# Seven-product weight forms by additions, two of them in transfers, and the scan's decay tiles for both heads of a feature block in one piece

## The chip, the cores and the metric

The kernel runs on one core of a Trainium2 chip, as one program of 52,322 recorded instructions. The metric is the device time of one execution in microseconds. The times shown for the kernel before are 2779.19 us (median of three), 2778.53 and 2781.94 us.

The engines are named as in the profile: PE is the matrix engine (PEld its weight loads), DVE the vector engine, ACT the scalar engine, POOL the GpSimd engine. SP issues transfers and computes nothing. Each engine works through its own list of instructions in order.

## What is computed

One residual block over 512 frames of 2048 channels. All operands are 32-bit floats.

```python
h = rmsnorm(x, norm1_w)
proj = einsum('bsd,de->bse', h, w_in)          # 2048 -> 22592 columns
q, k, v, g_ret, z, xbc, dt_raw, gate_r, gate_s = split(proj)
y_r = retention(q, k, v, positions) * silu(g_ret)
y_s = ssd(xbc, dt_raw, conv_w, conv_b, dt_bias, a_log, d_skip)
y_s = rmsnorm(y_s * silu(z), ssd_norm_w)
merged = sigmoid(gate_r) * (y_r @ w_br_ret) + sigmoid(gate_s) * (y_s @ w_br_ssd)
x = rmsnorm(x + merged @ w_out, norm_f_w)

# inside ssd, per chunk of frames (64 heads, 8 groups of B and C):
seg = acum[:, :, None] - acum[:, None, :]
decay = exp(where(causal, seg, -inf))
cb = einsum('blgn,bsgn->blsg', cc, bc)
y = einsum('blsg,blsgh,bsghp->blghp', cb, decay, xc)
```

## The kernel before

Nearly all of the work is the five big projections. Each is cut into **units** of 256 output columns by 512 frames over 2048 input channels. A unit is one call of `unit`, which calls `products`. There are 119 such units and a last one, written out by hand, which is done in two passes.

In a unit the 2048 channels are taken in eight steps of 256 (`k` in `range(NP)`). A step multiplies a 2 by 2 arrangement of 128x128 weight blocks by a 2 by 2 arrangement of 128x256 operand blocks. In 101 units (`SEVEN`) this is done with seven products of combined blocks in place of eight; in 18 units (`FOUR`, called plain) and the last one without combining. Each product is three matmuls on rounded halves (lines 202 to 204): high weights by high operand, high weights by low operand, low weights by high operand. A seven-product unit has 8 x 7 x 3 = 168 matmuls with 256 moving columns, a plain one 96 with 512.

Weights come in **pairs** of steps. One tile `wf` holds a pair: for each of its two steps seven slots of 128x128, of which slots 0 to 3 are loaded by SP (line 216, one transfer of 256 KB a step) and slots 4 to 6 are for combined blocks. In seven-product units DVE forms the combinations of both steps in three instructions: line 219 (two slots of each step, 128x512), then lines 221 and 222 (one slot of each step, 128x256 each). Then, for each step, ACT rounds the seven slots to `whi` (line 150) and DVE subtracts to get `wlo` (line 151). There are three buffers of `wf` (`FB`), seven of `whi` (`HB`), six of `wlo` (`LB`): a pair's load can be issued when the second `wlo` of the pair three before has been subtracted, and a rounding when PE is done with the weights seven steps before. All of this is issued at a higher priority than the work around it (`PRIO`), so the weights run ahead of PE. A scheduler fixes the order of each engine's list when the kernel is built.

The operand side (`operands`, with `combined` on POOL or DVE and `completed` on DVE) is formed in the same way, once for each projection: for `w_in` at the very start, where `POOL` forms combinations for seven of eight operand tiles, then for the branch outputs and the merged sum.

The stages, by the first loads of their weights: retention and its projections from the start to about 765 us, the SSD stage to about 2048 us, the three products of the branches to 2566 us, the output projection to the end.

In the SSD stage there are 32 feature blocks of 128 channels, that is, of two heads. For each head a tile `L` (128 x 4 x 128) is loaded with the running sums of that head spread over all partitions (line 643, one transfer of 256 KB), made into decays by ACT (four times line 645, once line 647), multiplied by `CB` on DVE (line 648), and used in four matmuls (line 650). These read 64 columns of weights, and the first head writes partitions 0 to 63 of the result, the second head 64 to 127. The hardware runs each of these matmuls as two, so a feature block has sixteen in the trace.

Of the kernel before, what the change touches and what calls it, by code (L numbers as in the profile page):

```python
# [16 lines left out]
P = 128  # L17
# [49 lines left out]
def constants():  # L67
# [7 lines left out]
    for h in range(NH):  # L75
# [17 lines left out]
SEVEN = (((0, 0, 1, 1), (1, 0, 3, 3), (1, 1, 0, 5)),  # L93
         ((2, 0, 5, 6), (2, 1, 4, 4)),
# [35 lines left out]
def hybrid_block(tc, A, out):  # L130
# [23 lines left out]
    def combined(f, eng):  # L154
        eng.tensor_tensor(f[:, 4, :], f[:, 0, :], f[:, 2, :], op=ALU.add)
        eng.tensor_tensor(f[:, 6, :], f[:, 0, :], f[:, 1, :], op=ALU.subtract)

    def completed(f, eng):
        eng.tensor_tensor(f[:, 5, :], f[:, 4, :], f[:, 1, :], op=ALU.subtract)
        eng.tensor_tensor(f[:, 0, :], f[:, 3, :], f[:, 5, :], op=ALU.subtract)  # L160
# [13 lines left out]
    def rows(src, i):  # L174
        return src[i * 256:(i + 1) * 256, :].rearrange("(r p) t -> p r t", p=P)

# [12 lines left out]
    def products(H, parts, pt, groups, PE=PE, after=None):  # L189
# [17 lines left out]
        for k in range(NP):  # L207
            with tc.high_priority(offset=PRIO):
                if k % 2 == 0:
# [8 lines left out]
                    if not plain:  # L218
                        DVE.tensor_tensor(f2[:, :, 4:6, :], f2[:, :, 1:3, :],  # L219
                                          f2[:, :, 0:1, :].to_broadcast([P, 2, 2, P]), op=ALU.subtract)  # L220
                        DVE.tensor_tensor(f2[:, :, 0, :], f2[:, :, 2, :], f2[:, :, 4, :], op=ALU.add)  # L221
                        DVE.tensor_tensor(f2[:, :, 6, :], f2[:, :, 3, :], f2[:, :, 0, :], op=ALU.subtract)  # L222
# [16 lines left out]
    def unit(H, parts, alt=False, plain=False):  # L239
# [7 lines left out]
        with tc.high_priority():  # L247
            if plain:
                for c in range(2):
                    ACT.copy(o[:, 2 * c:2 * c + 2, :], pt[2 * c][:, 0:1, :].to_broadcast([P, 2, 256]))  # L250
                    DVE.tensor_tensor(o[:, 2 * c, :], pt[2 * c][:, 1, :], o[:, 2 * c, :], op=ALU.add)
                    DVE.tensor_tensor(o[:, 2 * c:2 * c + 2, :], pt[2 * c + 1], o[:, 2 * c:2 * c + 2, :], op=ALU.add)
            else:
                p1, u = o[:, 0, :], o[:, 0:4:3, :]
                ACT.copy(p1, pt[0][:, 0, :])  # L255
                DVE.tensor_tensor(o[:, 1:3, :], pt[1], p1[:, None, :].to_broadcast([P, 2, 256]), op=ALU.add)  # L256
                DVE.tensor_tensor(u, o[:, 2:3, :].to_broadcast([P, 2, 256]), pt[2], op=ALU.subtract)
                DVE.tensor_tensor(o[:, 2, :], o[:, 0, :], pt[2][:, 1, :], op=ALU.subtract)
                DVE.tensor_tensor(u, pt[3], u, op=ALU.add)
# [297 lines left out]
    with tc.tile_pool(name="ssd", bufs=1) as sp:  # L557
# [30 lines left out]
        for g in range(NG):  # L588
# [14 lines left out]
            for jj in range(2):  # L603
# [5 lines left out]
                for e in range(2):  # L609
# [29 lines left out]
                    pi = att_tile()  # L639
                    for i in range(2):  # L640

                        L = sp.tile([P, TB, P], F32, name="L", bufs=2)
# [179 lines left out]
```

## Time and profile before

| | |
|---|---|
| median of three runs | 2779.19 us |
| the profiled execution | 2779.37 us |
| its span, first to last instruction | 2777.6 us |
| PE, DVE, ACT, POOL busy | 98%, 86%, 48%, 9% of the span |
| PE clock granted, mean | 0.991 |
| HBM read, written | 321.56 MB, 37.49 MB |
| packets of all transfer queues | 344,375 |

The profiled execution lies 1.8 us over its span and 0.2 us over the median, so sums made on the trace can be set against the median as they are. A matmul's duration in a row is from its entry to its modelled end, and matmuls overlap; the pace of PE is read from the distance of their starts. Rows of the timeline give start in us, duration in us, engine, line, operation, output and inputs by the program's names, and how many instructions a row merges. Rows by line and shape give count, busy us, mean ns of one, and the idle time just before them with what ended it. Rows of one stretch of time give each engine's busy us, the granted clock, the share of the 16 transfer engines' time that packets took, and GB/s.

### The profile page before, as it was taken

The numbers are of one execution on the slowest core, as the hardware profiler recorded it, in microseconds if no ns is written. First come the engines' busy times: TensorE is split into PE (matmuls) and PEld (weight loads), VectorE is DVE, ScalarE is ACT, GpSimd is POOL, SyncE is SP. The second block draws the span as 40 slices with busy tenths as digits, with TensorE's granted clock in tenths as the row PEclk, the third lists the DMA queues.
The fourth block names the chain that finished last, engine by engine and source line by source line (L and its number), as shares of the span: only waits on it lengthen the run. The fifth ranks groups of instructions, "written<-read, shape, count | busy, mean of one in ns | idle before, by whom it ended". The sixth has DMA issues, their size and how long they took to land.

```text
span 2777.6 us, 52322 instructions
## 1 busy us (share of the span) xinstructions
PE 2715.8 (98%) x20508; PEld 2586.4 (93%) x20508; DVE 2391.4 (86%) x3782; ACT 1336.1 (48%) x1905; POOL 253.1 (9%) x206
## 2 busy tenths in 40 slices
PE   6999999999999999999999999999999999999898
PEld 3899999999989999999999999999989989889797
DVE  8999888888869798898979899797989798898997
ACT  4344333333355555555565555465554343533453
POOL 4000000000000000000000000000021020111321
PEclk9999999999999999999999999999999999999999
DMA  3333333333333434343434434344465554556634
GB/s 125 99 103 104 97 109 103 103 92 103 103 111 114 134 122 133 104 128 117 135 121 135 135 109 126 119 129 120 129 199 168 162 179 137 167 179 194 217 117 137
DMA packets 344375, 362.48 MB, mean 131 GB/s; under 512 B 25664, under 2 KB 298304, under 8 KB 344128
## 3 DMA queue, kind: packets, MB, share of 16 engines
q1 hardware_dynamic: 323888, 325.32, 38.7%
q10 hardware_dynamic: 20240, 33.82, 3.3%
q8 instruction: 161, 2.64, 0.4%
q14 instruction: 86, 0.70, 0.1%
HBM read 321.56 MB, written 37.49 MB: 129 GB/s over the span
## 4 chain that ended last, share of the span: by engine, by line
PE 82%; DVE 8%; DMA 5%; issue 3%; ACT 1%; POOL 1%; SPq 0%; DVEq 0%; POOLq 0%; ACTq 0%
PE pb L204 23%; PE pb L203 23%; PE pb L202 23%; PE att L202 2%; PE att L204 2%; PE att L203 2%; DVE wlo L151 2%; PE att L650 2%; DMA wf<-in_w_in_dram 1%; PE att L536 1%; PE att L521 1%; DMA wf<-in_w_br_ssd_dram 1%; DVE hl L151 1%; PE pb L120 1%; PE att L654 1%
## 5 line engine op out<-in xcount | busy, mean ns | idle before, releaser
L203 PE MATMUL pb<-hl,whi 128*128 128x256 f32 (+1 forms) x5464 | 1601.1, 294 | 11.9 <-DVE hl L120 9.3
L202 PE MATMUL pb<-hh,whi 128*128 128x256 f32 (+1 forms) x5464 | 1596.8, 295 | 9.9 <-ACT hh L150 7.1
L204 PE MATMUL pb<-hh,wlo 128*128 128x256 f32 (+1 forms) x5464 | 1587.9, 294 | 6.0 <-DVE wlo L151 6.0
L150 ACT CAST whi<-wf 128x896 fp32r<-128x896 f32 (+1 forms) x968 | 824.5, 888 | 870.1 <-PE pb L203 396.6
L203 PEld LDWEIGHTS pb<-hl,whi 128*128 128x128 f32 x5464 | 1049.1, 192 | 34.6 <-DVE hl L120 11.0
L202 PEld LDWEIGHTS pb<-hh,whi 128*128 128x128 f32 x5464 | 1046.4, 192 | 33.8 <-ACT hh L150 8.4
L151 DVE TENSOR_TENSOR wlo<-wf,whi 128x896 fp32r<-128x896 f32 (+1 forms) x968 | 1011.8, 1056 | 71.9 <-PE pb L204 30.6
L204 PEld LDWEIGHTS pb<-hh,wlo 128*128 128x128 f32 x5464 | 1041.0, 192 | 28.1 <-DVE wlo L151 6.8
L219 DVE TENSOR_TENSOR wf<-wf 128x512 f32<-128x512 f32 x404 | 281.5, 697 | 159.1 <-DMA wf<-in_w_in_dram 118.8
L202 PE MATMUL att<-hh,whi 128*128 128x256 f32 (+1 forms) x768 | 227.0, 297 | 1.4 <-ACT whi L150 1.4
L203 PE MATMUL att<-hl,whi 128*128 128x256 f32 (+1 forms) x768 | 226.7, 297 | 0.0
L204 PE MATMUL att<-hh,wlo 128*128 128x256 f32 (+1 forms) x768 | 222.7, 297 | 2.0 <-DVE wlo L151 2.0
L221 DVE TENSOR_TENSOR wf<-wf 128x256 f32<-128x256 f32 x404 | 174.3, 432 | 4.0
L222 DVE TENSOR_TENSOR wf<-wf 128x256 f32<-128x256 f32 x404 | 174.0, 431 | 3.1
L202 PEld LDWEIGHTS att<-hh,whi 128*128 128x128 f32 x768 | 147.4, 192 | 6.0 <-ACT whi L150 2.0
L204 PEld LDWEIGHTS att<-hh,wlo 128*128 128x128 f32 x768 | 144.8, 191 | 7.0 <-DVE wlo L151 2.8
L203 PEld LDWEIGHTS att<-hl,whi 128*128 128x128 f32 x768 | 147.5, 192 | 3.9
L645 ACT ACTIVATE L<-L,sst 128x128 f32<-128x128 f32 x256 | 80.3, 394 | 70.3 <-DMA L<-A_d 40.6
L625 POOL TENSOR_TENSOR xl<-xd,sst 128x384 f32<-128x384 f32 x32 | 33.7, 1054 | 864.1 <-DVE xd L622 864.1
L255 ACT COPY o<-pb 128x256 f32<-128x256 f32 x89 | 33.0, 370 | 128.0 <-PE pb L204 117.8
L256 DVE TENSOR_TENSOR o<-pb,o 128x512 f32<-128x512 f32 x89 | 61.0, 685 | 36.2 <-PE pb L204 35.9
L542 POOL TENSOR_TENSOR rs<-rs,mhalf 128x1 f32<-128x1 f32 x32 | 23.9, 751 | 713.3 <-DVE rs L541 704.2
(230 smaller groups left out, 2133.4 us busy)
## 6 DMA issues: line engine op xcount, KB each, us to landing
wf<-in_w_in_dram SPq DMA_DIRECT2D x640, 256.0 KB, 3.1
wf<-in_w_br_ssd_dram SPq DMA_DIRECT2D x128, 256.0 KB, 3.5
wf<-in_w_out_dram SPq DMA_DIRECT2D x72, 256.0 KB, 3.2
wf<-in_w_in_dram SPq DMA_DIRECT2D x128, 128.0 KB, 2.5
L<-A_d SPq DMA_DIRECT2D x64, 256.0 KB, 3.4
wf<-in_w_br_ret_dram SPq DMA_DIRECT2D x64, 256.0 KB, 3.5
ys_d<-B ACTq DMA_DIRECT2D x32, 256.0 KB, 2.5
E<-E_d SPq DMA_DIRECT2D x64, 96.0 KB, 2.7
```

Source lines behind the costliest of these rows:

```text
L150: ACT.copy(dst_hi, src)
L151: DVE.tensor_tensor(dst_lo, src, dst_hi.bitcast(F32), op=ALU.subtract)
L202: PE.matmul(o, wh, xh, start=b not in started, stop=False, skip_group_check=True)
L203: PE.matmul(o, wh, xl, start=False, stop=False, skip_group_check=True)
L204: PE.matmul(o, wl, xh, start=False, stop=(k == NP - 1), skip_group_check=True)
L219: DVE.tensor_tensor(f2[:, :, 4:6, :], f2[:, :, 1:3, :], f2[:, :, 0:1, :].to_broadcast([P, 2, 2, P]), op=ALU.subtract)
L221: DVE.tensor_tensor(f2[:, :, 0, :], f2[:, :, 2, :], f2[:, :, 4, :], op=ALU.add)
L222: DVE.tensor_tensor(f2[:, :, 6, :], f2[:, :, 3, :], f2[:, :, 0, :], op=ALU.subtract)
L256: DVE.tensor_tensor(o[:, 1:3, :], pt[1], p1[:, None, :].to_broadcast([P, 2, 256]), op=ALU.add)
L625: POOL.tensor_tensor(xl, xd[:, :TB - 1], tail[:, :TB - 1, hs, None].to_broadcast([P, TB - 1, 2, 64]), op=ALU.mult)
L645: ACT.activation(L[:, c, :], L[:, c, :], AF.Relu, scale=-1.0, bias=At[:, c, h0 + i:h0 + i + 1])
L650: PE.matmul(pi[i * 64:(i + 1) * 64, c * P:(c + 1) * P], xd[:, c, i, :], L[:, c, :], start=True, stop=True)
```

## The change

It has four parts.

1. **Weight combinations.** The two sets of seven combinations (of weights and of operands) get other signs, so that on the weight side every combination is a sum. Slot 5 is loaded with a second copy of block 0 by a third transfer on SP's queue (new line 228, 128 KB for both steps). Then, for each step, one transfer issued by POOL (new line 230, `accum_op=ALU.add`) adds slots 1 and 2 into slots 0 and 5, within SBUF. DVE does the two that are left: slot 4 (new line 231) and slot 6 (new line 232), 128x256 each. The 128x512 instruction of line 219 is gone. Tables, signs on the operand side and signs where results are collected follow (`SEVEN`, `combined`, `completed`, `unit`, the last unit); their instructions keep engine and shape, except that in plain units ACT copies 256 columns in place of 512.
2. **Decay tiles.** `L` is one tile for both heads of a feature block, with one buffer, loaded in one transfer of 512 KB; the eight first activations are as before, the exponential and the product with `CB` are one instruction each over 1024 columns.
3. **Order of the matmuls on `L`.** The four positions are the outer loop and the two heads the inner one, so matmuls that write partitions 0 to 63 and 64 to 127 alternate.
4. **The order of the lists**, which the scheduler works out anew.

```diff
-SEVEN = (((0, 0, 1, 1), (1, 0, 3, 3), (1, 1, 0, 5)),
-         ((2, 0, 5, 6), (2, 1, 4, 4)),
+SEVEN = (((0, 0, 1, 1), (1, 0, 3, 3), (1, 1, 4, 5)),
+         ((2, 0, 5, 6), (2, 1, 0, 4)),
          ((3, 0, 6, 2), (3, 1, 2, 0)))
...
     def combined(f, eng):
-        eng.tensor_tensor(f[:, 4, :], f[:, 0, :], f[:, 2, :], op=ALU.add)
-        eng.tensor_tensor(f[:, 6, :], f[:, 0, :], f[:, 1, :], op=ALU.subtract)
+        eng.tensor_tensor(f[:, 4, :], f[:, 0, :], f[:, 2, :], op=ALU.subtract)
+        eng.tensor_tensor(f[:, 6, :], f[:, 0, :], f[:, 1, :], op=ALU.add)
...
+    def first_tiles(src, i):
+
+        return src[i * 256:(i + 2) * 256, :P].rearrange("(m r p) t -> p m r t", r=2, p=P)[:, :, 0, :]
...
                     if not plain:
-                        DVE.tensor_tensor(f2[:, :, 4:6, :], f2[:, :, 1:3, :],
-                                          f2[:, :, 0:1, :].to_broadcast([P, 2, 2, P]), op=ALU.subtract)
-                        DVE.tensor_tensor(f2[:, :, 0, :], f2[:, :, 2, :], f2[:, :, 4, :], op=ALU.add)
-                        DVE.tensor_tensor(f2[:, :, 6, :], f2[:, :, 3, :], f2[:, :, 0, :], op=ALU.subtract)
+
+                        SP.dma_start(out=f2[:, :, 5, :], in_=first_tiles(parts[0], k))
+                        for m in range(2):
+                            POOL.dma_start(out=f2[:, m, 0:6:5, :], in_=f2[:, m, 1:3, :], accum_op=ALU.add)
+                        DVE.tensor_tensor(f2[:, :, 4, :], f2[:, :, 0, :], f2[:, :, 2, :], op=ALU.add)
+                        DVE.tensor_tensor(f2[:, :, 6, :], f2[:, :, 4, :], f2[:, :, 3, :], op=ALU.add)
...
             if plain:
                 for c in range(2):
-                    ACT.copy(o[:, 2 * c:2 * c + 2, :], pt[2 * c][:, 0:1, :].to_broadcast([P, 2, 256]))
-                    DVE.tensor_tensor(o[:, 2 * c, :], pt[2 * c][:, 1, :], o[:, 2 * c, :], op=ALU.add)
+                    ACT.copy(o[:, 2 * c + 1, :], pt[2 * c][:, 0, :])
+                    DVE.tensor_tensor(o[:, 2 * c, :], pt[2 * c][:, 1, :], o[:, 2 * c + 1, :], op=ALU.subtract)
...
+                    L = sp.tile([P, 2, TB, P], F32, name="L")
+                    SP.dma_start(out=L.rearrange("p i c l -> p i (c l)"),
+                                 in_=A_d[hs, :].partition_broadcast(P))
                     for i in range(2):
-
-                        L = sp.tile([P, TB, P], F32, name="L", bufs=2)
-                        SP.dma_start(out=L.rearrange("p c l -> p (c l)"), in_=A_d[h0 + i].partition_broadcast(P))
                         for c in range(TB):
-                            ACT.activation(L[:, c, :], L[:, c, :], AF.Relu, scale=-1.0,
+                            ACT.activation(L[:, i, c, :], L[:, i, c, :], AF.Relu, scale=-1.0,
                                            bias=At[:, c, h0 + i:h0 + i + 1])
-                        ACT.activation(L, L, AF.Exp, scale=-1.0)
-                        DVE.tensor_tensor(L, L, CB, op=ALU.mult)
-                        for c in range(TB):
-                            PE.matmul(pi[i * 64:(i + 1) * 64, c * P:(c + 1) * P], xd[:, c, i, :], L[:, c, :],
+                    ACT.activation(L, L, AF.Exp, scale=-1.0)
+                    DVE.tensor_tensor(L, L, CB[:, None].to_broadcast([P, 2, TB, P]), op=ALU.mult)
+
+                    for c in range(TB):
+                        for i in range(2):
+                            PE.matmul(pi[i * 64:(i + 1) * 64, c * P:(c + 1) * P], xd[:, c, i, :], L[:, i, c, :],
                                       start=True, stop=True)
```

The scheduler's new lists at three places. First DVE's list in the products of the branches, where a unit of the second one begins; rows give line, operation, output and inputs with buffer numbers, so that a pair is known by the number of its `wf`. Before:

```order
L219 TENSOR_TENSOR wf_26146<-wf_26146 128x2x256
L151 TENSOR_TENSOR wlo_26068<-wf_26057,whi_26067 128x896
L221 TENSOR_TENSOR wf_26146<-wf_26146 128x2x128
L219 TENSOR_TENSOR wf_26202<-wf_26202 128x2x256
L222 TENSOR_TENSOR wf_26146<-wf_26146 128x2x128
L221 TENSOR_TENSOR wf_26202<-wf_26202 128x2x128
L222 TENSOR_TENSOR wf_26202<-wf_26202 128x2x128
L151 TENSOR_TENSOR wlo_26153<-wf_26146,whi_26152 128x896
L219 TENSOR_TENSOR wf_26258<-wf_26258 128x2x256
L151 TENSOR_TENSOR wlo_26178<-wf_26146,whi_26177 128x896
```

And the same pairs in the changed kernel, where they have other numbers and lines 231, 232 and 155 stand for the combinations and the subtraction:

```order
L231 TENSOR_TENSOR wf_26706<-wf_26706 128x2x128
L232 TENSOR_TENSOR wf_26706<-wf_26706 128x2x128
L155 TENSOR_TENSOR wlo_26715<-wf_26706,whi_26714 128x896
L155 TENSOR_TENSOR wlo_26740<-wf_26706,whi_26739 128x896
L231 TENSOR_TENSOR wf_26764<-wf_26764 128x2x128
L232 TENSOR_TENSOR wf_26764<-wf_26764 128x2x128
L155 TENSOR_TENSOR wlo_26773<-wf_26764,whi_26772 128x896
L231 TENSOR_TENSOR wf_26822<-wf_26822 128x2x128
L266 TENSOR_TENSOR o_26694<-att_26459,o_26694 128x512
L232 TENSOR_TENSOR wf_26822<-wf_26822 128x2x128
L267 TENSOR_TENSOR o_26694<-att_26460,o_26694 128x2x256
L155 TENSOR_TENSOR wlo_26798<-wf_26764,whi_26797 128x896
```

Before, the combinations of the second pair (26202) stood ahead of both subtractions of the first (26146); now both subtractions of the first (26706) stand ahead of the combinations of the second (26764), while the third pair's (26822) stand ahead of the second subtraction of the second.

Next POOL's list at the start, from its constants to its first work on the operands (`B8_215` is the second operand tile, `C7_224` the third). Before:

```order
L270 MEMSET mhalf_78 128x4
L286 MEMSET eps_91 128x1
L120 ISA
L120 TENSOR_TENSOR B8_215<-B8_215 128x256 x2
L120 TENSOR_TENSOR C7_224<-e_hl2_110,R1_81 128x512
L120 TENSOR_TENSOR C7_224<-C7_224 128x256 x2
```

After:

```order
L280 MEMSET mhalf_78 128x4
L296 MEMSET eps_91 128x1
L230 DMA wf_507<-wf_507 128x2x128 x2
L230 DMA wf_565<-wf_565 128x2x128 x2
L124 ISA
L124 TENSOR_TENSOR B8_215<-B8_215 128x256 x2
L124 TENSOR_TENSOR C7_224<-e_hl2_110,R1_81 128x512
```

Four adding transfers, for the first two pairs of the second unit, now stand ahead of the operand work, and so does the instruction printed as ISA stand behind them.

Last PE's list in the first SSD group, at the fourth feature block's products with `L`. Before, with the matmuls of its two heads (`L_9937`, `L_9949`) apart; the 20 rows left out between are products of units:

```order
L203 MATMUL pb1_9974<-hl6_290,whi_10130 128x256
L204 MATMUL pb1_9974<-hh6_277,wlo_10131 128x256
L202 MATMUL pb1_9974<-hh6_277,whi_10130 128x256
L650 MATMUL att_9936<-L_9937,xd_9922 64x128 x4
L203 MATMUL pb1_9974<-hl6_290,whi_10130 128x256
...
L203 MATMUL pb2_9975<-hl6_290,whi_10130 128x256
L650 MATMUL att_9936<-L_9949,xd_9922 64x128 x4
L204 MATMUL pb2_9975<-hh6_277,wlo_10131 128x256
```

After, with one tile `L_10197`:

```order
L211 MATMUL pb2_10231<-hl5_284,whi_10382 128x256
L212 MATMUL pb2_10231<-hh5_266,wlo_10383 128x256
L210 MATMUL pb2_10231<-hh6_277,whi_10394 128x256
L663 MATMUL att_10196<-L_10197,xd_10182 64x128 x8
L667 MATMUL att_10217<-A8_8835,S_10190 128x128 x3
L211 MATMUL pb2_10231<-hl6_290,whi_10394 128x256
```

All eight now stand together, and the merged row hides that the heads alternate in it.

14 lines of the change are left out of this document (7 added, 7 removed).

## The prediction

> **What bounds the kernel now.** I read first the shares of the engines on the page, then the windows by stage, to see where PE is not full.
>
> ```profile
> PE 2715.8 (98%) x20508; PEld 2586.4 (93%) x20508; DVE 2391.4 (86%) x3782; ACT 1336.1 (48%) x1905; POOL 253.1 (9%) x206
> 850.00:2040.00 1190.00, 1189.03 (x9364) 1149.42 (x9364) 1031.42 (x1647) 680.38 (x1081) 78.91 (x62) 1.00 0.42 125
> 2040.00:2200.00 160.00, 157.10 (x1123) 148.00 (x1122) 143.37 (x213) 71.06 (x86) 20.50 (x20) 0.99 0.56 179
> 2200.00:2380.00 180.00, 177.86 (x1294) 168.14 (x1294) 147.58 (x211) 73.41 (x89) 18.21 (x15) 1.00 0.51 161
> 2380.00:2560.00 180.00, 170.98 (x1221) 162.04 (x1220) 159.76 (x227) 69.58 (x83) 31.37 (x22) 0.98 0.58 183
> 2560.00:2700.00 140.00, 132.86 (x911) 123.68 (x910) 129.74 (x174) 66.45 (x82) 36.64 (x24) 0.96 0.53 172
> ```
>
> PE idles 1.0 us in the 1190 us of the SSD stage, and 2.9 + 2.1 + 9.0 + 7.1 = 21.1 us from 2040 to 2700. A busy PE may still be slow, so I look at its pace in the timeline.
>
> ```profile
> 449.90 0.28 PE L202 MATMUL pb<-hh,whi 128*128 128x256 f32 x1
> 450.02 0.28 PE L203 MATMUL pb<-hl,whi 128*128 128x256 f32 x1
> ```
>
> One matmul of a unit starts every 0.12 us, without gaps. A seven-product pair has 42 of them: 5.04 us. **PE sets the time**; what DVE does counts only where PE waits for it, and the waits say how much that is.
>
> ```profile
> PE pb L204 <- DVE wlo L151: 6.0, 4, 3.3
> ACT whi L150 <- PE pb L203: 396.6, 173, 7.0
> SPq L216 <- DVE wlo L151: 1244.9, 335, 11.6
> ```
>
> PE waited 6.0 us for weights from DVE in its main form, while ACT waited 396.6 us for PE to free weight buffers: weights run ahead. The loads wait for buffers 335 times: the three `wf` buffers are always in use.
>
> **The change, part by part.** *DVE's work.* Per pair the 128x512 instruction goes.
>
> ```profile
> L219 DVE TENSOR_TENSOR wf<-wf 128x512 f32<-128x512 f32 x404 | 281.5, 697 | 159.1 <-DMA wf<-in_w_in_dram 118.8 <-DMA wf<-in_w_br_ssd_dram 25.3 <-DMA wf<-in_w_br_ret_dram 8.0
> L221 DVE TENSOR_TENSOR wf<-wf 128x256 f32<-128x256 f32 x404 | 174.3, 432 | 4.0
> L151 DVE TENSOR_TENSOR wlo<-wf,whi 128x896 fp32r<-128x896 f32 x808 | 894.5, 1117 | 46.7 <-ACT whi L150 21.6 <-PE pb L204 19.1 <-ACT o L584 3.5
> L150 ACT CAST whi<-wf 128x896 fp32r<-128x896 f32 x808 | 728.4, 941 | 731.5 <-DVE wf L222 314.9 <-PE pb L203 291.4 <-issue 39.2
> ```
>
> 404 x 0.697 = 281.5 us leave DVE, which falls to about 2110 us (76%). Beside a full PE that is worth nothing. It can take back PE's waits for DVE's weights, 6.0 us, most likely where DVE is fullest, after 2040 (580.5 of 660 us, 88%); the bounds are 0 and the 21.1 us of idle there. I take **-5**, near the 6.0 and below it, because the transfers below take some back.
>
> *The matmuls on `L`.* Here PE itself gets shorter. In the trace the sixteen matmuls of a feature block come in one run or in two of eight, here the first and last of each kind and the row that follows, and the second run of sixteen:
>
> ```profile
> 867.47 1.58 PE L650 MATMUL att<-L,xd 128*64 128x128 f32 x16
> 868.98 0.39 PE L204 MATMUL pb<-hh,wlo 128*128 128x256 f32 x1
> ...
> 880.52 1.58 PE L650 MATMUL att<-L,xd 128*64 128x128 f32 x16
> ...
> 926.15 1.09 PE L650 MATMUL att<-L,xd 128*64 128x128 f32 x8
> 927.17 0.39 PE L203 MATMUL pb<-hl,whi 128*128 128x256 f32 x1
> ...
> 1884.68 1.09 PE L650 MATMUL att<-L,xd 128*64 128x128 f32 x8
> 1885.69 0.49 PE L654 MATMUL att<-A,S 128*128 128x128 f32 x2
> ...
> 2039.61 1.58 PE L650 MATMUL att<-L,xd 128*64 128x128 f32 x16
> 2041.12 0.49 PE L654 MATMUL att<-A,S 128*128 128x128 f32 x2
> ```
>
> Eight take PE 1.02 us (927.17 - 926.15), but sixteen take 1.51: the second head's eight add 0.49, so about half of them ran beside the first head's, which write the other 64 partitions. There are 25 runs of sixteen and 14 of eight (25 x 16 + 14 x 8 = 512): 25 x 1.51 + 14 x 1.02 = 52.0 us. With the heads alternating, each matmul has a partner behind it. The bounds for a block are 1.02 (all beside) and 2.03 (none). I take 1.1, near the lower, because the overlap in the runs of sixteen was got without alternating: 32 x 1.1 = 35 us, **-17**. PE is the bound in that stage, so this shows in the time.
>
> The chain to these matmuls gets longer, as both heads are now made together.
>
> ```profile
> L<-A_d SPq DMA_DIRECT2D x64, 256.0 KB, 3.4
> A<-ys_d SPq DMA_DIRECT2D x6, 512.0 KB, 3.7
> L645 ACT ACTIVATE L<-L,sst 128x128 f32<-128x128 f32 x256 | 80.3, 394 | 70.3 <-DMA L<-A_d 40.6 <-DVE B L656 11.3 <-PE pb L203 10.3
> L647 ACT ACTIVATE L<-L 128x512 f32<-128x512 f32 x64 | 40.3, 632 | 0.2
> L648 DVE TENSOR_TENSOR L<-L,A 128x512 f32<-128x512 f32 x64 | 47.5, 756 | 6.1 <-ACT L L647 5.7
> ```
>
> With one buffer the load waits for the block before: 3.7 for 512 KB + 8 x 0.39 + at most 2 x 0.63 + 2 x 0.76 = 9.6 us, and loads of weights stand behind that wait on SP. The two blocks of a pair follow each other at 13.05 us (867.47, 880.52), filled with a unit's matmuls. I take 0; without that cover PE would lose what is over 13 us.
>
> *The new transfers.* Per pair: one more issue on SP, two on POOL, and DVE's first combination waits for both. POOL's column shows 9% busy, and no transfer issued by POOL is in the trace, so I bound it by the nearest rows.
>
> ```profile
> L216 SPq DMA_DIRECT2D wf<-in_w_in_dram x768: 367/462/1797, 5.8 to 2037.0; - x192
> L625 POOL TENSOR_TENSOR xl<-xd,sst 128x384 f32<-128x384 f32 x32 | 33.7, 1054 | 864.1 <-DVE xd L622 864.1
> L732 POOL TENSOR_TENSOR R<-R,o 128x512 f32<-128x512 f32 x13 | 28.5, 2193 | 103.4 <-ACT o L731 80.7 <-ACT R L729 22.3
> wf<-in_w_in_dram SPq DMA_DIRECT2D x640, 256.0 KB, 3.1
> wf<-in_w_in_dram SPq DMA_DIRECT2D x128, 128.0 KB, 2.5
> mm_d<-f ACTq DMA_DIRECT2D x14, 256.0 KB, 4.5
> ```
>
> Issue on POOL: 0.4 us (as on SP) to 2.2 (POOL's longest group); I take 1.05, its middling one. Landing: 2.5 (a load of that size) to 4.5 (the slowest row); I take 2.5. Let X be the time from a freed buffer to both additions landed: two SP issues and the landing of the 256 KB load, 0.46 + 3.1, with the third transfer 0.92 + 2.5, so about 3.8 with the semaphores; then two POOL issues and a landing. X is 3.8 + 0.8 + 2.5 = 7.1 at best, **8.4** as taken, 3.8 + 4.4 + 4.5 = 12.7 at worst.
>
> Three buffers go round. From landing, a pair needs two combinations (0.43 each), a rounding (0.94) and two subtractions (1.12 each): 4.0 us until its buffer is free. By DVE's new list in the branches the round is closed over three pairs where both subtractions stand ahead of the next combinations (4.0 + X), and over two where the next pair's combination stands ahead of a subtraction (1.5 + X); one with two more combinations between costs 4.9 + X. Eight pairs hold one of each: 3X + 10.4. At 8.4 that is 4.5 us a pair against PE's 5.04, hidden; at 12.7 it is 6.1. **It decides at X = 10.** In the SSD stage, with more PE work between (about 765 to 2048 us for 224 pairs, 5.7 us a pair), it decides near 11.7.
>
> The Trainium skill (DMA: Bandwidth & Descriptors, Anatomy of one DMA) gives a transfer issued by GpSimd about 2.0 us fixed plus its bytes at 436 GB/s, 2.3 us for 128 KB, an estimate by that page; X would be some 0.2 us shorter than mine and the sum the same. No run here shows it yet.
>
> *The start.* POOL makes operand combinations on the path to the first units.
>
> ```profile
> 29.04 1.97 POOL L120 TENSOR_TENSOR B<-B 128x256 f32<-128x256 f32 x2 [28.18 <-DVE B L120]
> 63.13 3.93 POOL L120 TENSOR_TENSOR B<-B 128x256 f32<-128x256 f32 x2 [1.63 <-DVE B L120]
> 29.21 1.22 DVE L219 TENSOR_TENSOR wf<-wf 128x512 f32<-128x512 f32 x1
> L120 POOLq MODIFY_POOL_CONFIG  x2: 11/11/11, 0.8 to 0.8; - x2
> ```
>
> The second pair of weights was there by 29.2, and now its additions stand ahead of POOL's work at 29.04: two issues more, 0.8 to 4.4 us, on a chain that then goes on to 67 us. I take **+3**. The configuring instruction, at 0.8 us until now, moves behind them to about 30 us.
>
> The Trainium skill (GPSIMD Engine Reference, Instruction dispatch) says the first call after it also loads code, about 6 us; in this trace the first call, 28 us later, shows no such time. By that rule the start would lose 6 us more and the sum be 2766.
>
> All else keeps engine and shape and lies on engines that wait; the shorter copy in plain units falls to ACT, 48% busy.
>
> **Sum.** From the profiled execution's 2779.4: -17 - 5 + 3 = -19, **2760 us**.
>
> **The rivals.** *Additions late* (slower): X above 10.5 eats all gains, since 19 us over the 96 seven-product pairs after 2048 are 0.2 us a pair. At 12.7 those lose 96 x 1.02 and the 308 before them 308 x 0.36, with the matmuls' gain hidden: 2779 + 98 + 111 = 2988; between, at 11.5, it is 96 x 0.57 and 2779 - 17 + 3 + 55 = 2820. For it: SP's loads, POOL's list and DVE's list are all in order, so one late addition holds everything behind it. Against: six `wlo` buffers hold three pairs, 15 us of PE's work, against a single delay. Chance 0.19.
>
> *The transfer engines fill.*
>
> ```profile
> q1 hardware_dynamic: 323888, 325.32, 38.7%
> ```
>
> A packet of 1 KB took 0.387 x 16 x 2777.6 / 323888 = 53 ns. A pair adds 256 load packets of half that size (27 ns) and 512 adding packets, read twice and written once, between 27 and 106 ns: 1.3 to 3.8 us on each engine. At 53 ns it is 2.1 us, 42 points of 5.04: 0.58 becomes 1.00 in 2380 to 2560. At 106 even the SSD stage's 0.42 becomes 1.09 (3.8 of 5.7 us is 67 points): 9% of its 1283 us alone, about 2895. Chance 0.11, mostly about 2800.
>
> *The matmuls on `L` don't pair when alternated*: 2.03 a block, 65 us in place of 52: 2779 + 13 - 5 + 3 = 2790. Against: the runs of sixteen above. Chance 0.06.
>
> *DVE is freed and nothing else happens*, the start and fuller queues taking back what the matmuls give: 2774 to 2785. Chance 0.12.
>
> **How the numbers follow.** The forecast, 2750 to 2772, has 0.52. Measurements of this kernel can tell about 0.2% (5.6 us) from no change: faster 0.53, same 0.14, slower 0.33. The range, 2745 to 2860, reaches over the lower half of the slow cases; the likeliest case's own is 2750 to 2772.
>
> **What would show it.** Sixteen matmuls on `L` in 1.0 to 1.15 us: the third step right; 1.5 or more: wrong. POOL's issue and the landing of its transfers put together to X: under 10, and no wait of PE for `wlo` in the SSD stage; over it, waits of DVE's first combination for the adding transfer, and pairs at more than 5.04 us after 2048. POOL's first tensor operation at 32 us, or at 38 if code is loaded there. The transfer share of 2380 to 2560 below 0.95. The prediction falls if PE idles more than 20 us between 200 and 2040.

## The result and the profile after

| kernel | median, us | runs | ratio to before, 95% interval |
|---|---|---|---|
| before, beside it | 2778.86 | 4 | |
| changed | 4144.34 | 4 | 1.4911 [1.4893, 1.4929] |

The changed kernel takes half as long again, 1365 us more; the prediction was 2760, with 2860 as its upper end. First the page of the changed kernel: shares of the engines, the granted clock in 40 slices, and the two largest transfer queues (packets, MB, share of the 16 engines).

```profile
PE 3105.8 (75%) x20508; PEld 2911.3 (70%) x20508; DVE 2135.1 (51%) x3346; ACT 1314.9 (32%) x1869; POOL 1198.5 (29%) x1014
...
PEclk8988888888888888888888888888898888988888
...
q1 hardware_dynamic: 429168, 378.29, 30.8%
q0 software_dynamic: 219776, 105.96, 22.1%
```

No engine is full now. PE falls from 98 to 75%, DVE by 256 us, and the clock in every slice but a few stands at 8 tenths. Next, the windows by stage (start to end, length, then busy us of PE, PEld, DVE, ACT and POOL, the clock, the transfer share, GB/s), here the SSD stage and the `ssd` branch:

```profile
1150.00:3090.00 1940.00, 1457.48 (x9986) 1389.90 (x9987) 985.03 (x1548) 718.34 (x1117) 530.32 (x445) 0.85 0.54 120
...
3335.00:3850.00 515.00, 377.59 (x2376) 351.12 (x2376) 268.28 (x380) 138.07 (x166) 162.49 (x135) 0.86 0.64 156
```

The loss is spread evenly: PE idles a quarter of the time in a stage where it idled 1.0 of 1190 us before, and the transfer engines are little over half busy. What is waited for stands in the waits (who waits for whom, us in all, times, longest):

```profile
POOL wf L230 <- issue: 1673.1, 617, 6.1
ACT whi L154 <- DVE wf L232: 1587.8, 233, 19.2
DVE wf L231 <- issue: 1226.1, 290, 7.8
DVE wf L231 <- DMA wf<-wf: 443.7, 109, 10.7
...
PE pb L210 <- ACT o L265: 225.8, 40, 10.7
...
PE pb L212 <- DVE wlo L155: 96.0, 34, 6.6
```

ACT waits for DVE's combinations, DVE for POOL's additions, and POOL before 617 of 808 additions for nothing that the profile shows. PE itself waits only 250.8 us for weights (`whi` and `wlo`, 96.0 us of it in the last row), and 495.5 us for ACT or DVE to collect a unit's results (`o`, lines 261 to 269). This fits lists in order: where ACT or DVE stands before a late pair, its other work behind that comes late too. POOL's timeline in the retention stage shows the wait before its additions:

```profile
600.01 1.21 POOL L230 DMA_DIRECT2D wf<-wf  x1 [2.27 <-issue]
603.51 1.22 POOL L230 DMA_DIRECT2D wf<-wf  x1 [2.29 <-issue]
607.44 1.21 POOL L230 DMA_DIRECT2D wf<-wf  x1 [2.72 <-issue]
...
623.13 1.21 POOL L230 DMA_DIRECT2D wf<-wf  x1 [2.24 <-issue]
623.88 1.74 POOL L552 TENSOR_TENSOR rs<-rs,mhalf 128x1 f32<-128x1 f32 x1
```

An addition takes POOL 1.21 us, then some 2.2 us or more pass before the next. POOL is not blocked: at 623.88 a tensor instruction starts 0.75 us after an addition did. Only another addition has to wait. Of the 807 distances between additions none is under 3.427 us, and 394 lie between that and 3.6. The row of the line, with the time from issue to landing:

```profile
L230 POOL DMA_DIRECT2D wf<-wf x808: 1191/1210/1336, 27.5 to 4090.8; - x162
...
DMA to landing us min/median/max: 3.1/3.2/7.8
```

The distance is about the landing time, and set one by one against the landings it is exact: no addition starts before the one ahead has landed, and 679 of 807 start within 0.4 us after it (0.32 us in the median). **One addition is in flight at a time**. Now one pair through SP and DVE:

```profile
591.28 0.88 SPq L224 DMA_DIRECT2D wf<-in_w_in_dram  x2
592.20 0.47 SPq L228 DMA_DIRECT2D wf<-in_w_in_dram  x1
...
622.44 0.88 SPq L224 DMA_DIRECT2D wf<-in_w_in_dram  x2
```
```profile
603.27 0.42 DVE L231 TENSOR_TENSOR wf<-wf 128x256 f32<-128x256 f32 x1 [3.88 <-DMA wf<-wf]
...
610.69 0.42 DVE L231 TENSOR_TENSOR wf<-wf 128x256 f32<-128x256 f32 x1 [3.44 <-DMA wf<-wf]
...
619.23 0.42 DVE L231 TENSOR_TENSOR wf<-wf 128x256 f32<-128x256 f32 x1 [4.93 <-issue]
...
621.33 1.08 DVE L155 TENSOR_TENSOR wlo<-wf,whi 128x896 fp32r<-128x896 f32 x1
```

The pair's loads go out at 591.28 (its additions are those at 603.51 and 607.44). Its first combination runs at 610.69, 19.4 us later; its last subtraction (621.33, ends at 622.41) stands behind the *next* pair's first combination (619.23), which waits for its own additions; 0.03 us after it the buffer is loaded again. So I split every pair, in every run (the runs are described under the experiments), into **X** (first load to first combination) and the **rest** (to the end of its last subtraction). For the 188 seven-product pairs of the SSD stage, means from these rows (in all_by_dve and dve_no_third to DVE's first instruction on the pair, in half_by_dve to the first that needs POOL's addition too):

| run | X | rest | (X + rest) / buffers | median us |
|---|---|---|---|---|
| before | 4.5 | 13.1 | 5.8 | 2779 |
| changed | 16.6 | 11.1 | 9.2 | 4144 |
| hb6_ring4k | 11.8 | 8.5 | 6.8 | 3198 |
| fb4_ring4k | 11.8 | 17.0 | 7.2 (of 4) | 3260 |
| pool_copies | 10.2 | 8.8 | 6.3 | 2971 |
| half_by_dve | 9.8 | 11.4 | 7.1 | 3242 |
| order_ring1k | 19.7 | 5.6 | 8.4 | 3898 |
| order_ring4k | 13.4 | 5.6 | 6.3 | 2951 |
| order_copies | 12.4 | 5.8 | 6.1 | 2814 |
| order_fb4 | 19.0 | 6.4 | 6.4 (of 4) | 2885 |
| all_by_dve | 5.1 | 13.0 | 6.0 | 2825 |
| dve_no_third | 4.3 | 13.0 | 5.8 | 2770 |

In all of them a freed buffer is loaded again after 0.03 to 0.08 us (mean), so the fourth column is the time a pair takes. Where PE sets the pace it is 5.8 us, and the rest is mostly waiting for PE. The column tells where a pair's time lies; as buffers are reloaded at once in every run, it does not by itself tell what sets the pace.

PE's timeline at two places of the SSD stage, with matmuls of a unit and with those on `L`:

```profile
1502.73 0.41 PE L210 MATMUL pb<-hh,whi 128*128 128x256 f32 x1
1502.95 0.41 PE L211 MATMUL pb<-hl,whi 128*128 128x256 f32 x1
```
```profile
1512.99 1.09 PE L663 MATMUL att<-L,xd 128*64 128x128 f32 x16
1514.01 0.38 PE L212 MATMUL pb<-hh,wlo 128*128 128x256 f32 x1
1514.24 0.28 PE L210 MATMUL pb<-hh,whi 128*128 128x256 f32 x1
1514.35 0.28 PE L211 MATMUL pb<-hl,whi 128*128 128x256 f32 x1
```

Sixteen take 1.02 us (1514.01 - 1512.99), in all 32 blocks. And a product matmul of 256 columns that took 0.12 us before takes 0.21 in stretches of the changed kernel: 2976 of them are followed by the next after 0.20 to 0.23 us, against 196 before. The windows of the two places above, with the granted clock as the third number from the end:

```profile
1499.20:1512.80 13.60, 10.88 (x49) 10.61 (x49) 7.64 (x13) 3.60 (x6) 5.66 (x5) 0.50 0.47 84
1512.90:1526.40 13.50, 9.17 (x84) 8.70 (x82) 6.62 (x13) 5.35 (x13) 3.85 (x4) 1.00 0.63 141
```

In the trace the clock is granted either whole or half, and the mean of 0.851 is a mixture of the two: of the 2976 slow matmuls 2819 start while it is half. They cost PE some 2780 x 0.09 us = 250 us of busy time. How much of that lengthens a kernel whose PE also idles for 1040 us (4146.2 - 3105.8) is not shown.

### The profile page after: what moved, and what is told of

Its sections match the earlier page's. It is cut to its first block, busy times and chain, and to the rows that moved or that the text cites. A ratio compares the mean times of both kernels' runs of the same rounds, so it can differ in the third digit from the quotient of the medians.

```text
span 4146.2 us, 55337 instructions
## 1 busy us (share of the span) xinstructions
PE 3105.8 (75%) x20508; PEld 2911.3 (70%) x20508; DVE 2135.1 (51%) x3346; ACT 1314.9 (32%) x1869; POOL 1198.5 (29%) x1014
## 3 DMA queue, kind: packets, MB, share of 16 engines
q0 software_dynamic: 219776, 105.96, 22.1%
## 5 line engine op out<-in xcount | busy, mean ns | idle before, releaser
L210 PE MATMUL pb<-hh,whi 128*128 128x256 f32 (+1 forms) x5464 | 1740.9, 321 | 503.6 <-ACT o L265 225.8
L212 PE MATMUL pb<-hh,wlo 128*128 128x256 f32 (+1 forms) x5464 | 1714.5, 317 | 96.0 <-DVE wlo L155 96.0
L230 POOL DMA_DIRECT2D wf<-wf x808 | 980.2, 1213 | 2699.2 <-issue 1673.1
L211 PE MATMUL pb<-hl,whi 128*128 128x256 f32 (+1 forms) x5464 | 1723.5, 316 | 37.2 <-DVE hl L124 18.6
L210 PEld LDWEIGHTS pb<-hh,whi 128*128 128x128 f32 x5464 | 1173.6, 215 | 560.3 <-ACT o L265 235.6
L212 PEld LDWEIGHTS pb<-hh,wlo 128*128 128x128 f32 x5464 | 1167.9, 215 | 125.6 <-DVE wlo L155 103.2
L211 PEld LDWEIGHTS pb<-hl,whi 128*128 128x128 f32 x5464 | 1176.2, 215 | 62.1 <-DVE hl L124 22.1
L155 DVE TENSOR_TENSOR wlo<-wf,whi 128x896 fp32r<-128x896 f32 (+1 forms) x968 | 991.8, 1040 | 154.2 <-ACT whi L154 103.5
L639 PE MATMUL att<-xl,A 128*128 128x128 f32 x192 | 41.1, 371 | 86.1 <-POOL xl L635 86.1
L667 PE MATMUL att<-A,S 128*128 128x128 f32 x192 | 41.5, 320 | 77.3 <-DVE S L646 75.1
L639 PEld LDWEIGHTS att<-xl,A 128*128 128x128 f32 x192 | 36.3, 275 | 89.1 <-POOL xl L635 89.1
```

The source lines that it names most:

```text
L155: DVE.tensor_tensor(dst_lo, src, dst_hi.bitcast(F32), op=ALU.subtract)
L210: PE.matmul(o, wh, xh, start=b not in started, stop=False, skip_group_check=True)
L211: PE.matmul(o, wh, xl, start=False, stop=False, skip_group_check=True)
L212: PE.matmul(o, wl, xh, start=False, stop=(k == NP - 1), skip_group_check=True)
L230: POOL.dma_start(out=f2[:, m, 0:6:5, :], in_=f2[:, m, 1:3, :], accum_op=ALU.add)
L639: PE.matmul(ps[:, c * P:(c + 1) * P], Bk[:, c, :], xl[:, c].rearrange("p i d -> p (i d)"), start=True, stop=True)
```

## The experiments

Where an edit changes which instructions there are, or their order, the scheduler works out all lists anew, so such a run differs from its control in more than the edit. Two comparisons are free of this: among hb6_ring1k, hb6_ring2k and hb6_ring4k, and between pool_copies and the changed kernel, the traces show the same sequence of operations on PE, DVE, POOL and SP.

### One addition at a time

The kernel sets aside 1024 bytes of each SBUF partition for the descriptors of POOL's transfers. A larger piece needs room, so the control gives up a `whi` buffer.

```
-FB, HB, LB = 3, 7, 6                     (both)
+FB, HB, LB = 3, 6, 6
-... dynamic_dma_scratch_size=1024        (hb6_ring4k; hb6_ring2k: 2048)
+... dynamic_dma_scratch_size=4096
```

> The changed kernel with six `whi` buffers in place of seven, as the control for the next run, which needs the room. Every theory: 4100 to 4250 us, POOL's adding transfers never less than 3.43 us apart, as in the changed kernel's trace.

> The control with 4096 in place of 1024 bytes a partition set aside for the descriptors of transfers that POOL issues (`dynamic_dma_scratch_size`). Theory 'one at a time': at 1024 only one adding transfer has room, so the next issue waits until the one before is done (1.21 us + 2.25 us of waiting); with 4096 the two of a pair go out 1.2 to 1.3 us apart, the pair no longer costs POOL 7 us, and the time falls below 2900 us. Rival 'issue': POOL itself needs 3.43 us to make a transfer; the gaps and about 4150 us stay. Rival 'transfer engines': the packets were the limit; gaps may shrink, but the share of the transfer engines rises to over 0.9 and the time stays above 3300 us. Rival 'latency': the round over three buffers is too long even with both additions in flight, about 3.8 + 2.4 + 3.2 = 9.4 us and 4 us of work; time 2780 to 2900 with gaps of 1.2 us.

> 2048 bytes in place of 4096, six `whi` buffers. If 1024 have room for one addition, 2048 have room for two: the two of a pair go out 0.73 us apart and the time is within 2% of the run with 4096, 3140 to 3260 us. If an addition takes more than half of 2048: 3.43 us between them and 4160 us.

Measured: 4160.27 us (1.4975 [1.4945, 1.5005]), 3197.98 (1.1496 [1.1463, 1.1528]) and 3214.78 (one run). POOL's timeline of hb6_ring4k:

```profile
605.62 4.95 POOL L230 DMA_DIRECT2D wf<-wf  x4 [3.80 <-DMA wf<-in_w_in_dram]
612.75 1.09 POOL L552 TENSOR_TENSOR rs<-rs,mhalf 128x1 f32<-128x1 f32 x2 [2.18 <-DVE rs L551]
614.06 2.45 POOL L230 DMA_DIRECT2D wf<-wf  x2 [0.22 <-issue]
```

Two additions of a pair now start 0.73 us apart (median), four take 4.95 us of POOL, and waiting before an addition for nothing visible is gone from the head of the waits. A number in one line is worth 962 us. The wait was for room, not POOL's own work nor the transfer engines. 2048 bytes do nearly as well: the two of a pair go out 0.74 us apart, and up to three are under way at once, where 1024 bytes hold one. The Trainium skill (SBUF — State Buffer, SBUF size: 192, 224, or 256?) sets 16 KiB of a partition aside for these descriptors. The Trainium skill (DMA: Bandwidth & Descriptors, Anatomy of one DMA) says of generating descriptors that many can be emitted before it costs anything; here the cost was not in generating them but in room for them, 3.43 us at the least from one addition to the next with 1024 bytes.

The expected "below 2900" was wrong: with X at 11.8 the pair still takes 6.8 us.

```
-POOL.dma_start(out=f2[:, m, 0:6:5, :], in_=f2[:, m, 1:3, :], accum_op=ALU.add)
+POOL.dma_start(out=f2[:, m, 0:6:5, :], in_=f2[:, m, 1:3, :])
```

> The same transfers from POOL as plain copies: slots 0 and 5 get slots 1 and 2 themselves instead of having them added, so the products are of other numbers. Theory 'one at a time' with the space taken by what an addition needs over a copy (its target is read too): copies go out closer than 3.43 us, 1.2 us where two stand together, and the time is below 3000 us. If the wait belongs to any transfer that POOL issues: gaps of 3.4 us and about 4100 us.

Measured: 2970.86 us (one run), at 1024 bytes. The queue's row:

```profile
q0 software_dynamic: 38784, 105.96, 10.9%
```

Copies go out 0.72 us apart, up to three of them under way at once, so the room is taken by what an addition needs over a copy. Same bytes, but 38,784 packets in place of 219,776, and 0.109 x 2969.1 / 404 = 0.8 us of every transfer engine a pair in place of 0.221 x 4146.2 / 404 = 2.3.

### Nothing issued by POOL, and the third load

```
-for m in range(2):                        (all_by_dve)
-    POOL.dma_start(out=f2[:, m, 0:6:5, :], in_=f2[:, m, 1:3, :], accum_op=ALU.add)
+DVE.tensor_tensor(f2[:, :, 0:6:5, :], f2[:, :, 0:6:5, :], f2[:, :, 1:3, :], op=ALU.add)
```
```
-SP.dma_start(out=f2[:, :, 5, :], in_=first_tiles(parts[0], k))        (dve_no_third, in place of that)
-...
+DVE.tensor_tensor(f2[:, :, 5, :], f2[:, :, 0, :], f2[:, :, 2, :], op=ALU.add)
+DVE.tensor_tensor(f2[:, :, 0, :], f2[:, :, 0, :], f2[:, :, 1, :], op=ALU.add)
```

> Only POOL's two adding transfers are undone: DVE adds slots 1 and 2 into slots 0 and 5 with one 128x512 instruction; the third load, the new signs and the feature block's decays stay. If POOL's transfers are the whole cause: 2750 to 2775 us (before less 17 for the matmuls on `L`, DVE's load as before, and one more 128 KB load a pair). If another part of the change costs time as well, the third load or the new order: the part of it above 2780 is that.

> The run with all additions on DVE took 2825 us, some 60 more than that was expected to. Here its third load of a pair goes too: DVE forms slot 5 from slots 0 and 2 and slot 0 from 0 and 1 (two 128x256 instructions in place of one 128x512). If the third load (0.46 us on SP a pair, 53 MB, and a longer X) is what the 60 us are: 2760 to 2780. If they come from the signs or the feature block's decays: 2815 to 2830, as before this step.

Measured: 2825.37 us (1.0174 [1.0149, 1.0198]) and 2769.63 (0.9968 [0.9958, 0.9979]). Without POOL's transfers 1319 of the 1365 us are back. Taking out the third load as well, with DVE's other form of the additions and the new lists, gives 56 more and puts the kernel 0.3% ahead of before; the prediction gave this load nothing but a longer X. X grows only from 4.3 to 5.1 us with it. The engines' shares, first without the third load, then with it:

```profile
PE 2701.4 (98%) x20508; PEld 2570.6 (93%) x20508; DVE 2409.4 (87%) x4154; ACT 1329.8 (48%) x1878; POOL 256.6 (9%) x206
```
```profile
PE 2713.7 (96%) x20508; PEld 2572.1 (91%) x20508; DVE 2377.3 (84%) x3750; ACT 1333.2 (47%) x1878; POOL 252.0 (9%) x206
```

PE idles 106 us with it (2819.9 - 2713.7) and 66 without (2767.9 - 2701.4). DVE has more to do in the faster kernel. Where the idle comes from stands in the waits, first with the third load, then without it:

```profile
DVE wf L229 <- DMA wf<-in_w_in_dram: 219.0, 182, 3.7
...
PE att L666 <- DVE S L645: 10.5, 14, 2.3
PE pb L210 <- DVE o L265: 8.0, 8, 2.7
```
```profile
DVE wf L228 <- DMA wf<-in_w_in_dram: 103.5, 124, 2.6
```

In the SSD stage (760 to 2075 us and 760 to 2030) PE waits 36.7 us with the load and 2.7 without it, and of the 36.7 only 0.9 are for weights: most are for the scan's state `S` and for a unit's results `o`, which DVE makes. DVE stands twice as long before the first instruction of a pair, and what is behind it in its list comes late. That the one makes the other is argued and not shown, since the lists differ too.

### The decays alone

l_only is before with the change's feature block and nothing else; alt_only is before with its two tiles, two loads and all, and only the matmuls reordered:

```
+Ls = []
 for i in range(2):
     ...
-    for c in range(TB):
-        PE.matmul(pi[i * 64:...], xd[:, c, i, :], L[:, c, :], ...)
+    Ls.append(L)
+for c in range(TB):
+    for i in range(2):
+        PE.matmul(pi[i * 64:...], xd[:, c, i, :], Ls[i][:, c, :], ...)
```

> The kernel before with the feature block's decays of the change alone (one `L` tile, one load, alternating heads). In the changed kernel's trace sixteen matmuls on `L` take 1.02 us in all 32 blocks, where before they took 52.0 us in all: 19 us less of PE. Theory 'PE's bound': 2758 to 2765 us, PE's idle in the SSD stage as before (about 5 us). Rival 'longer chain': with one `L` buffer the chain to these matmuls is late at times, PE idles 20 to 40 us more in the SSD stage, as it did with all additions on DVE, and the time is 2775 to 2800.

> The kernel before with nothing but the order of the sixteen matmuls on `L` changed: both heads' `L` are formed as before, in two tiles with two loads, and the matmuls alternate between them. If alternating is what makes them short: 1.02 us for sixteen as in the changed kernel, PE busy 2697 us, and 2760 to 2770 us, no worse than the run with the whole decay change (2767.9). If forming both at once matters too, or waiting for the second head's tile costs PE time: 2770 to 2780.

Measured: 2767.88 us (0.9961 [0.9949, 0.9974]) and 2769.91 (0.9975 [0.9964, 0.9987]). The page of l_only, and its group of these matmuls (count, busy us, mean ns):

```profile
PE 2697.1 (98%) x20508; PEld 2566.2 (93%) x20508; DVE 2389.9 (86%) x3750; ACT 1343.9 (49%) x1884; POOL 268.9 (10%) x206
```
```profile
L653 PE MATMUL att<-L,xd 128*64 128x128 f32 x512 | 35.0, 279 | 1.1 <-issue 1.1
```

PE is busy 2715.8 - 2697.1 = 18.7 us less; the time falls by 0.4%, some 10 us, and lies 3 us above what the theory expected. PE idles 8.5 us in the SSD stage (1271.51 busy of 1280) in place of 4.5 (1285.50 of 1290). In alt_only PE is busy 2708.9 us, not the 2697 expected: in 16 of the 32 blocks two matmuls run ahead of the other fourteen, 0.36 + 1.02 us, since the second head's tile comes later. One tile for both heads gives the rest of the 18.7, but in time the two kernels' intervals overlap. l_only has the lowest median of this study, ahead of both kernels; the intervals of alt_only and dve_no_third overlap its own.

### More buffers, fewer additions

```
-FB, HB, LB = 3, 7, 6                                       (fb4_ring1k; fb4_ring4k with 4096 bytes)
+FB, HB, LB = 4, 5, 5
```
```
-for m in range(2):                                         (half_by_dve)
-    POOL.dma_start(out=f2[:, m, 0:6:5, :], in_=f2[:, m, 1:3, :], accum_op=ALU.add)
+POOL.dma_start(out=f2[:, 0, 0:6:5, :], in_=f2[:, 0, 1:3, :], accum_op=ALU.add)
+DVE.tensor_tensor(f2[:, 1, 0:6:5, :], f2[:, 1, 0:6:5, :], f2[:, 1, 1:3, :], op=ALU.add)
```

> The changed kernel with four `wf` buffers in place of three (five `whi` and five `wlo` make the room). Theory 'one at a time': POOL still cannot issue two additions less than 3.43 us apart, 808 x 3.43 = 2771 us if nothing else ever held one up, and a pair needs 6.9 us against PE's 5.04, so the time stays above 3400 us. Rival 'only latency': with a fourth buffer the round of 15.8 us (freed buffer to first combination) and 4.5 us of work is closed in 20.3 / 4 = 5.1 us a pair, and the time falls to 2850 us or less.

> Four `wf` buffers and 4096 bytes a partition for the descriptors. With three buffers and 4096 bytes the trace shows 11.6 us from freed buffer to first combination (median) and pairs every 5.4 to 5.8 us. If that round over three buffers is what remains: (11.6 + 4.5) / 4 = 4.0 us a pair, under PE's 5.04, and 2770 to 2860 us, near the run with all additions on DVE. Rival 'order': POOL's, DVE's and SP's lists hold each other up whatever the buffers; above 3050 us.

> The changed kernel with one of a pair's two additions left to POOL and the other done by DVE (one 128x256 instruction), 1024 bytes as in the change. Theory 'one at a time': 404 additions of 3.43 us are 1386 us, so POOL hardly waits for itself; X falls from 16 us to about 0.9 + 4.6 + 3.2 = 8.7 and the time to 2850 to 3000. If what costs is the number of adding packets or of loads and not their succession: half of the loss stays, about 3480.

Measured: 4172.53 us (1.5021 [1.4993, 1.5048]), 3259.97 (1.1724 [1.1702, 1.1746]), 3241.63 (1.1672 [1.1646, 1.1697]). A fourth buffer gives nothing at either size. In fb4_ring4k X stays at 11.8 us and the rest doubles to 17.0. This does not rule out latency over three buffers: the room came from `whi` and `wlo`, and ACT now waits 566.9 us for PE to free a `whi`, against 176.9 in hb6_ring4k. In half_by_dve X is 9.8, near the 8.7 expected, yet the rest is 11.4 and the time 240 us over its range. The two misses point to the rest: work standing in the engines' lists. half_by_dve's first waits:

```profile
POOL wf L229 <- DVE wf L230: 1046.5, 151, 27.0
ACT whi L154 <- DVE wf L232: 827.9, 221, 15.4
```

By the profile POOL's additions wait for DVE's list, and ACT for DVE.

### DVE's order

One edge is added, a rule for the scheduler that one instruction stands behind another: a pair's first combination behind both subtractions of the pair before, on DVE. The scheduler's other lists change with it.

```
-DVE.tensor_tensor(f2[:, :, 4, :], f2[:, :, 0, :], f2[:, :, 2, :], op=ALU.add)
+first = DVE.tensor_tensor(f2[:, :, 4, :], f2[:, :, 0, :], f2[:, :, 2, :], op=ALU.add).ins
+if last_lo:
+    tc.add_manual_dep(first, last_lo[-1], mybir.DependencyInfo(mybir.DependencyClass.NoSync, ...), ...)
```

> The run with 4096 bytes and six `whi` buffers, with one order fixed in addition: DVE's first combination of a pair stands behind both `wlo` subtractions of the pair before it. In that run a buffer was held 11.7 us from its first load to the first combination and 8.7 us from there to its last subtraction, and reloaded 0.03 us later: 20.4 us for three pairs, 6.8 us each. The 8.7 are 4.0 us of work, the rest is waiting in lists. Theory 'order': DVE stands before the next pair's first combination, which waits for its additions, while a subtraction that would free a buffer is queued behind; with the order fixed that part falls to 4.5 to 5.5 us, the pair to 5.4 to 5.7 us, and the time to 2850 to 3000. Rival 'round': the waits only move elsewhere, the buffer is held as long, and the time stays at 3150 to 3250.

> The changed kernel (1024 bytes, seven `whi` buffers) with DVE's order fixed as before: the first combination of a pair behind both `wlo` subtractions of the pair ahead. In the changed kernel a buffer is held 16.5 us to the first combination and 11 from there. Theory 'order adds to succession': the 11 fall to about 5 us, (16.5 + 5) / 3 = 7.2 us a pair, just above the 6.9 us that two additions need one after the other, and at some 400 pairs by 2 us less the time falls by about 800 us to 3250 to 3450. Rival 'succession alone sets the pace': POOL was the limit all along, the pair stays near 9 us, and the time above 4000 us.

> The changed kernel with DVE's order fixed and POOL's transfers as plain copies (slots 0 and 5 get slots 1 and 2 themselves, so the products are of other numbers); 1024 bytes. Without the order fixed, copies took 10.2 us to the first combination and 8.8 from there, 6.3 us a pair, 2971 us. With it, if the round decides: (10.2 + 5) / 3 = 5.1 us, PE's own pace, and 2800 to 2860 us; if X grows as the rest shrinks, as it did with additions: 2900 or more.

> The run with 4096 bytes and DVE's order fixed, with four `wf` buffers (five `whi`, five `wlo`). With three the buffer was held 13.4 + 5.6 us, 6.3 us a pair. If the round over three buffers is what remains: (13.4 + 5.6) / 4 = 4.8 us, under PE's pace, and 2830 us or less. If fewer `whi` and `wlo` buffers or the third load and the packets hold it: 2900 to 3100.

Measured: 2950.68 us (1.0615 [1.0590, 1.0640]), 3898.47 (1.4036 [1.3995, 1.4077]), 2813.81 (one run), 2885.49 (1.0389 [1.0359, 1.0419]). With 4096 bytes the order, with the lists that come of it, is worth 247 us: the rest falls from 8.5 to 5.6, X grows by 1.6, so the time came as expected but the pair, 6.3 us, not (5.4 to 5.7). With 1024 bytes it is worth 246, not the 800 expected, since X grows from 16.6 to 19.7. There the succession itself is the limit:

```profile
POOL wf L232 <- issue: 1938.2, 657, 6.9
```
```profile
1499.13 1.22 POOL L232 DMA_DIRECT2D wf<-wf  x1 [2.23 <-issue]
...
1502.63 1.21 POOL L232 DMA_DIRECT2D wf<-wf  x1 [1.42 <-issue]
1508.14 1.22 POOL L232 DMA_DIRECT2D wf<-wf  x1 [4.30 <-issue]
1513.28 1.21 POOL L232 DMA_DIRECT2D wf<-wf  x1 [3.91 <-DMA wf<-in_w_in_dram]
```

An addition with its wait takes 1.21 + 1938.2 / 657 = 4.16 us on average, not 3.43, and a pair of two 8.3: the 8.4 of the table. (3.43 is the quickest; the wait reaches 6.9.) 781 of 807 additions start within 0.4 us after the landing of the one before, and landings take 3.9 us in the mean. The fourth buffer gives 65 us more, less than expected: X grows to 19.0, and ACT now waits 243.4 us for PE to free one of five `whi`. Copies with the order fixed reach 2814 at X = 12.4: the time of the first case, though X did grow as in the second.

## Why the prediction was wrong, step by step

**What bounds the kernel**: right for before. PE was the bound, and more work on DVE cost nothing there: dve_no_third gives DVE 18 us more than before and is 0.3% faster.

**DVE's 281.5 us**: the line left, and DVE's busy time fell by 256.3 us (2391.4 to 2135.1). What that is worth, and whether the -5 came, can't be seen under the loss.

**The matmuls on `L`**: right. 1.02 us in place of the 1.1 taken, PE 18.7 us less in place of 17. In time about 10: PE idles 6.8 us more in all (68.6 in place of 61.8), 4.0 of them in the SSD stage. Whether the longer chain, for which the prediction says "I take 0", makes these 4.0 was not tested.

**The new transfers: the step that failed**, in three places.

1. "Then two POOL issues and a landing." The form was wrong: with 1024 bytes the second addition waits for the landing of the first, and a pair's first for those of the pair before. Both ends of the range of X held that two transfers overlap, so it came to 16.6 us against 12.7 "at worst". Its parts, means over the same 188 pairs (an addition's issue, 1.05 as taken, counts to the row after it):

   | part of X | taken | changed | hb6_ring4k |
   |---|---|---|---|
   | first load to first addition | 3.8 | 8.6 | 5.9 |
   | to the second addition | 1.05 | 3.9 | 0.7 |
   | to its landing | 3.55 | 4.1 | 4.7 |
   | to the first combination | 0 | 0.1 | 0.4 |

   hb6_ring4k shows the cause: only room is added, and 962 us are back. Issue (1.21 us) and landing (3.2 in the median) lay within their bounds but above what was taken, the third load landed in 4.0 in place of 2.5, and with room enough X is still 11.8, past the 10 at which the sum decides. The line with 1024 stood in the kernel, and no row of before had a transfer issued by POOL.
2. "Eight pairs hold one of each: 3X + 10.4." The price of the lists was wrong: the rest is 8.5 us at X = 11.8, where the three cases allow 4.0, 1.5 and 4.9. At 11.8 that sum gives about 2840; it was 3198. With the order fixed it errs the other way: at 12.4, the copies, it gives about 2930, and 2814 was measured. The sum asked only when weights come; in the traces PE waits longer for other work of ACT and DVE behind the late pairs.
3. The third load was one more 0.46 us on SP and a longer X. Without it, and with DVE's additions in another form and the lists made anew, 56 us are back.

**The rivals.** "Additions late" is what happened, in kind; its dearest case was 2988, as it had no additions one after the other. Its reason against, 15 us of PE's work in six `wlo` buffers, covers one late addition and not every one. "The transfer engines fill" did not: 0.54 and 0.64 in the windows above, though a pair's adding packets alone take 2.3 us of each engine, inside the 1.3 to 3.8 given. "The matmuls don't pair" is refuted, "nothing happens" too.

**The start.** POOL's first tensor operation comes at 38.85 us, the time given for code loading. It is not that:

```profile
27.52 1.33 POOL L230 DMA_DIRECT2D wf<-wf  x1 [26.64 <-DMA wf<-in_w_in_dram]
31.03 1.23 POOL L230 DMA_DIRECT2D wf<-wf  x1 [2.18 <-issue]
34.49 1.21 POOL L230 DMA_DIRECT2D wf<-wf  x1 [2.23 <-issue]
38.00 1.22 POOL L230 DMA_DIRECT2D wf<-wf  x1 [2.30 <-issue]
38.85 1.90 POOL L124 TENSOR_TENSOR B<-B 128x256 f32<-128x256 f32 x2
```

Four additions stand ahead, one after the other, where the prediction counted two. The configuring instruction runs at 38.7 us, and the operation right behind it takes 1.90 us where it took 1.97. In hb6_ring4k it starts at 31.69 us (2.7 us later than before, where +3 was taken) and takes 3.22. The Trainium skill's 6 us for loading code at a first call (GPSIMD Engine Reference, Instruction dispatch) show in neither trace. My sign for it would have been misread: two causes shared one time.

**What stays open**: how much of the 56 us is the third load and how much the new lists, the same for the 247 us of the order, what the slower matmuls cost in time, and what holds order_fb4 60 us over all_by_dve.

## What to carry to other kernels

Before a transfer is given to a queue that the kernel has not used, ask what each engine needs for the *next* one: a queue's succession (here 3.4 to 4.2 us, set by the room for descriptors) bounds a loop as its latency does, and a range made only of latencies does not contain it. A scheduler that places a consumer early in an in-order list turns a late transfer into a stop for everything behind it; one ordering edge, with the lists it led to, was worth 247 us. Work moved off an engine that waits anyway may buy nothing, so a change that pays only there should be split: here one part was worth 10 us and the other cost over 1300.

## What the runs showed of the hardware

- Room for descriptors sets how many adding transfers are in flight. At 1024 bytes a partition a 128 KB SBUF-to-SBUF addition of 512-byte pieces excludes the next until it has landed; at 2048 two go 0.74 us apart; plain copies of the same shape go 0.72 us apart at 1024. POOL's tensor instructions run on meanwhile.
- An addition moves in packets of one piece of 512 bytes: 219,776 packets for 105.96 MB, against 38,784 for copies, and 2.8 times the transfer engines' time a pair.
- Alternating matmuls that write partitions 0 to 63 and 64 to 127 run side by side: sixteen in 1.02 us, as eight of one half alone.
- With PE idle a quarter of the time, the granted clock falls from 0.991 to 0.851 in the mean, in stretches of half the clock; there a matmul of 256 columns takes 0.21 us in place of 0.12.
